# K and V made by the last pair of each gate phase, their memory lent to folds, kept parts and loads; T2 and B21 of the head k tile by k tile

## The chip, the cores and the metric

The kernel runs on one core of one Trainium2 chip. The metric is the device time of one execution in microseconds; it is given as a median of several runs. The core has five engines that run side by side and wait for each other by semaphores: PE (TensorE, matrix products, which write to the PSUM banks), DVE (VectorE), ACT (ScalarE), POOL (GpSimd), and SP (SyncE, which here only issues DMAs). Each engine works through its own queue in order, so an instruction that waits holds up what is queued behind it on its engine.

## The reference

One layer of a decoder trunk over 2048 rows of width 1024:

```python
mod = jax.nn.silu(c) @ w_ada[l] + b_ada[l]
shift, scale, gate = jnp.split(mod, 3, axis=-1)
u = x * (1.0 + scale[:, None, :]) + shift[:, None, :]
h = u @ w_in[l]
q, k, v, a_gate, p_in, p_gate, m_a, m_p = jnp.split(h, offsets, axis=-1)
a = sliding_window_sink_attention(q, k, v, sinks[l], bias, mask) * jax.nn.silu(a_gate)
a = a @ w_attn_proj[l]
p = jnp.einsum('bsgc,gcd->bsgd', multiscale_causal_pool(p_in), w_pool_mix[l]).reshape(B, S, POOL_WIDTH)
p = (p * pool_scale[l]) * jax.nn.silu(p_gate)
p = p @ w_pool_proj[l]
y = jax.nn.sigmoid(m_a) * a + jax.nn.sigmoid(m_p) * p
y = (y @ w_out[l]) * (1.0 + gate[:, None, :])
x = layer_norm(DEEPNORM_ALPHA * x + y, ln_gain[l], ln_bias[l])
```

Attention has 16 query heads, 2 key and value heads of width 64 (so K and V are 128 columns each of `h`), and a causal window of 128 rows. All arrays are float32.

## The kernel before

**Precision and products.** A float32 operand is split into a high part (rounded, type fp32r, made by an ACT copy) and a low part (the rest, made by a DVE subtraction, the helper `low`, line 131). A product is three matmuls: high by high, high by low, low by high (`mm3`).

**Sets and quads.** The 2048 rows are worked in two halves of 1024 rows (s = 0, 1), and each half as two column chunks of 512. Large products go by seven block products in place of eight (a Strassen-Winograd scheme). The moving side is kept as seven *sets* of four k tiles, each k tile split: B11, B21, B22 (blocks of u), and the sums T1, T2, T3, T4. The stationary side is a *quad* (class `Quad`): two column blocks of weights, 2 x 1024 wide, loaded into a buffer W (three thirds; two buffers) and a buffer A22 (two buffers in a common pool, and two of the phase's own that every other group uses). POOL makes the sums of weights (`sum1` line 283, `mid` lines 287 to 289, `late` line 293). A quad is worked in two steps. `front` splits the first pair of weights and does B11 and T1. `back` splits the second pair and does T2 and B21, splits the third pair and does T3 and B22, and last T4. `pair_split` (line 315 is its ACT copy, line 131 its DVE subtraction) writes to two of the four `w_set` slots, a ring; a slot comes free when the matmuls that read it are done. Each of the four result blocks goes to the quad's `consume`.

**Gate phases.** The gate phase of a half makes K, V and the gates: 17 quads, worked in groups of two (`gate_quads`); one late group has a single quad. `ring` runs the groups: `back` of a group, then `front` of the next. After each product it calls `tick`, and hooks given for a group and a position (`steps`, `at`) emit other work there: a full group has 14 ticks, ten in `back` and four in `front`. In the first phase the hooks are: the fold of the pool weights (`fold_parts`, for four groups: fetch, split, products, keep: `w_pool_mix` is folded into the pool columns of `w_in`, and stored), the sets of the second half (`sums_to`: x is loaded into two `spare` tiles, modulated, summed on POOL, split part by part into `k_hi` and `k_lo`, and stored), the last part of the modulation (`gate_modulation`) and the spreading of the bias. The fold's split also takes two `w_set` slots per half. `spare` is a ring of two tiles; `k_hi`, `k_lo`, gates and other pieces share the ring `c` of five.

**K and V.** The quad of K and V is the first of each phase. K is copied and split into the tile `kk` by `take_k` (line 651 its ACT copies, 64 partitions each), with four copies and four subtractions per chunk. V is kept as `vt`, and turned by PE into the tile `vv` in `turn_v`, emitted as `turn(0)` and `turn(1)` at hooks of group 0. The last piece of a phase, `first_q`, makes the first block of q for both chunks; then attention for that half begins, and it reads `kk` and `vv`. Attention also works on the first pair of the next phase at its end (`fill_one`).

**The head.** `head` runs before the first phase. For each of eight k tiles k it loads the modulation weights and x, makes shift (small PE products) and scale (a DVE reduction) in `opening(k)`, modulates x (`modulate_x`), writes the parts of B11 or B21 (`middle(k)`), and of T1 or T2 (`closing(k)`). B11 and T1 of the first two quads are done k tile by k tile as the parts come (`products`); T2 and B21 of these quads come later, in `back` of group 0. `rest_sums` makes the raw sums for T3 and T4; their parts and those of B22 are split in three hooks (`rest`) at group 0, positions 0, 1 and 3. The memory of `kk` and `vv` (18 KB and 9 KB per partition) holds weights and x of the head at first (`head_kk`, `head_vv`).

**What sets the order.** Operations on `pe`, `act`, `dve`, `pool` and `sp` keep the order of the program among themselves; those on `nc.scalar`, `nc.vector` and the like are placed by the planner of the framework by its own estimate of what is ready. The planner also puts in the waits. Memory that a pool gives out under one name again is given when its last users are done.

## Time and profile before

| | us |
|---|---|
| median of 3 runs | 1823.36 (1822.94 to 1827.17) |
| the profiled execution | 1824.69 |
| its span | 1822.9 |
| PE busy in the span | 1722.4 |
| DVE busy | 1315.4 |
| ACT busy | 933.8 |
| POOL busy | 929.5 |

The head lasts until about 73 us, the first gate phase until 439, the first attention until 706, the second gate phase from there to about 1040, the second attention to about 1322, and the projections and the output product take the rest. A line of the timeline gives start, duration (both in us), engine, line of the kernel, operation, output and inputs, shape, how many instructions are taken together, and in brackets the idle time ahead of it with what ended it. L55 is the line of the wrapper through which all operations on `pe`, `act`, `dve`, `pool` and `sp` go. A line of the waits gives the total in us, the number of waits, and the longest. The names `set_B` and `set_T` stand for all sets of that letter.

### The profile page before, as it was taken

The numbers are of one execution on the slowest core, as the hardware profiler recorded it, in microseconds if no ns is written. First come the engines' busy times: TensorE is split into PE (matmuls) and PEld (weight loads), VectorE is DVE, ScalarE is ACT, GpSimd is POOL, SyncE is SP. The second block draws the span as 40 slices with busy tenths as digits, with TensorE's granted clock in tenths as the row PEclk, the third lists the DMA queues.
The fourth block names the chain that finished last, engine by engine and source line by source line (L and its number), as shares of the span: only waits on it lengthen the run. The fifth ranks groups of instructions, "written<-read, shape, count | busy, mean of one in ns | idle before, by whom it ended". The sixth has DMA issues, their size and how long they took to land. (4 is left out here: it accounts for less than half of the span.)

```text
span 1822.9 us, 25301 instructions
## 1 busy us (share of the span) xinstructions
PE 1722.4 (94%) x8248; PEld 1432.9 (79%) x8248; DVE 1315.4 (72%) x2290; ACT 933.8 (51%) x1965; POOL 929.5 (51%) x758
## 2 busy tenths in 40 slices
PE   6789899999999999999999999999989999999996
PEld 6678787878888887777777888888877778777775
DVE  6967676644777787787666467777848897877887
ACT  4644344445777776444444377777724343423451
POOL 2245454551356567635445125357744875576552
PEclk9899999999999999999999999999999999999998
DMA  9265667656344468676676724453876575688442
GB/s 358 94 213 184 224 218 236 241 208 168 122 162 145 165 223 299 234 262 242 243 262 236 254 80 148 156 172 129 300 271 220 196 254 184 211 312 349 150 156 87
DMA packets 164003, 381.32 MB, mean 209 GB/s; under 512 B 19728, under 2 KB 23840, under 8 KB 163872
## 3 DMA queue, kind: packets, MB, share of 16 engines
q1 hardware_dynamic: 150528, 342.17, 53.7%
q0 software_dynamic: 10112, 33.06, 5.2%
q10 hardware_dynamic: 3232, 4.49, 0.9%
q8 instruction: 65, 1.06, 0.2%
q14 instruction: 66, 0.54, 0.1%
HBM read 244.35 MB, written 138.44 MB: 210 GB/s over the span
## 5 line engine op out<-in xcount | busy, mean ns | idle before, releaser
L55 PE MATMUL mm<-set_B,w_set 128*128 128x512 f32 x3240 | 802.1, 396 | 22.2 <-DVE w_set L131 22.0
L55 PEld LDWEIGHTS mm<-set_B,w_set 128*128 128x128 f32 x3240 | 602.9, 189 | 154.0 <-DVE w_set L131 30.3
L55 PE MATMUL lg<-set_T,w_set 128*128 128x512 f32 x2088 | 521.9, 400 | 44.3 <-DVE w_set L131 16.7
L55 PEld LDWEIGHTS lg<-set_T,w_set 128*128 128x128 f32 x2088 | 396.0, 192 | 146.2 <-DVE w_set L131 27.0
L131 DVE TENSOR_TENSOR w_set<-W,w_set 128x1024 fp32r<-128x1024 f32 x162 | 241.9, 1493 | 130.3 <-ACT w_set L315 125.6
L315 ACT CAST w_set<-W 128x1024 fp32r<-128x1024 f32 x162 | 169.2, 1049 | 242.5 <-PE mm L55 134.1
L55 PE MATMUL mm<-set_T,w_set 128*128 128x512 f32 x1080 | 266.4, 395 | 0.0
L55 PEld LDWEIGHTS mm<-set_T,w_set 128*128 128x128 f32 x1080 | 201.3, 189 | 41.6
L293 POOL TENSOR_TENSOR W<-W 128x512 f32<-128x512 f32 x56 | 80.0, 1429 | 151.0 <-DVE w_set L131 142.3
L287 POOL TENSOR_TENSOR W<-W 128x512 f32<-128x512 f32 x56 | 87.2, 1556 | 125.2 <-DVE w_set L131 99.9
L366 POOL TENSOR_TENSOR p<-p,u 128x512 f32<-128x512 f32 x58 | 100.6, 1736 | 87.3 <-DVE u L365 79.4
L55 DVE TENSOR_TENSOR o<-pv,o 64x128 f32<-64x128 f32 x256 | 72.4, 283 | 93.2 <-ACT o L55 90.5
L55 ACT ACTIVATE L<-L,nm 128x257 f32<-128x257 f32 (+1 forms) x256 | 127.1, 498 | 8.4 <-DVE nm L55 3.3
L283 POOL TENSOR_TENSOR W<-W,A 128x512 f32<-128x512 f32 x56 | 82.7, 1476 | 86.9 <-DMA W<-in_win_dram 20.2
L55 DVE TENSOR_TENSOR k_lo<-spare,k_hi 128x512 fp32r<-128x512 f32 x88 | 92.4, 1058 | 47.8 <-ACT k_hi L55 24.0
L55 DVE CUSTOM_DVE_ANT_0 L<-lg,bt,nsink 128x256 f32<-128x256 f32 (+1 forms) x256 | 111.6, 473 | 5.3 <-PE lg L55 1.3
L288 POOL TENSOR_TENSOR W<-W 128x512 f32<-128x512 f32 x56 | 90.4, 1614 | 15.1 <-DMA W<-in_win_dram 12.3
L55 POOL TENSOR_TENSOR w_set<-W,w_set 128x1024 fp32r<-128x1024 f32 x14 | 33.7, 2405 | 122.8 <-ACT w_set L55 89.7
L55 POOL TENSOR_TENSOR p<-nxt,pg 128x512 f32<-128x512 f32 x32 | 41.3, 1291 | 104.6 <-DVE sm L55 104.6
L55 ACT COPY o<-pv 64x256 f32<-64x256 f32 x128 | 47.3, 370 | 82.3 <-PE pv L55 80.2
L55 DVE TENSOR_TENSOR ptl<-pt,pth 128x512 fp32r<-128x512 f32 (+1 forms) x128 | 85.7, 669 | 1.7 <-ACT pth L55 1.6
L55 ACT CAST k_hi<-spare 128x512 fp32r<-128x512 f32 x88 | 53.4, 615 | 60.4 <-POOL spare L55 32.3
(207 smaller groups left out, 2507.2 us busy)
## 6 DMA issues: line engine op xcount, KB each, us to landing
W<-in_win_dram SPq DMA_DIRECT2D x68, 256.0 KB, 4.1
w_set<-wmix_d SPq DMA_DIRECT2D x32, 512.0 KB, 5.4
A<-in_win_dram SPq DMA_DIRECT2D x34, 256.0 KB, 5.1
W<-in_win_dram POOLq DMA_DIRECT2D x34, 256.0 KB, 3.6
ag_d<-sig SPq DMA_DIRECT2D x32, 256.0 KB, 3.5
pg_d<-sig SPq DMA_DIRECT2D x32, 256.0 KB, 3.6
ma_d<-sig SPq DMA_DIRECT2D x32, 256.0 KB, 4.1
mp_d<-sig SPq DMA_DIRECT2D x32, 256.0 KB, 3.7
```

The source lines that it names most:

```text
L55: return lambda *args, **kw: self.tc.keep_in_program_order(op(*args, **kw))
L131: engine.tensor_tensor(dst, src, as32(hi), ALU.subtract)
L283: e.tensor_tensor(self.w[:, 1, :], self.w[:, 2, :], self.a22, ALU.add)
L287: e.tensor_tensor(x[:, 1, :], x[:, 1, :], x[:, 0, :], ALU.subtract)
L288: e.tensor_tensor(x[:, 2, :], x[:, 0, :], x[:, 2, :], ALU.subtract)
L293: e.tensor_tensor(x[:, 0, :], x[:, 0, :], x[:, 1, :], ALU.subtract)
L315: a.copy(by_two(hi), raw)
L366: nc.gpsimd.tensor_tensor(p5, p5, u2, ALU.add)
```

## The change

The quad of K and V goes from the first place of a gate phase to the last group, beside the last gate quad. Group 0 is then two quads of the attention gate. `turn(0)` is emitted at position 7 of the last group, `turn(1)` inside `first_q`, between its two products. In the first phase the memory of `kk` and `vv` is a set of rooms until then: the fold's splits of the weights are written there and no more to `w_set`; two of three kept parts (`k_hi`, `k_lo`) go there and no more to the ring `c`; and two more `spare` tiles are taken there, in turn with the two of the ring. `place_kv` ends that when the first block of K is consumed. The fold of a group has its products two ticks behind its splits. The ticks of folds, of the first sums and of the gate modulation are shifted.

In the head, the second pairs are split earlier, and T2 and B21 of both quads are done as their k tiles come. The copies of two results (`u2`, `p5`) are made there too. The parts of T3 are split in the head, those of B22 and T4 at positions 4 and 6 of group 0, and the `late` sum of the second quad at position 4.

```diff
         def split():
-            t.extend(ph.c(n, F32R) for n in ("k_hi", "k_lo"))
+            at = ph.turn_of("parts")
+            if at:
+                t.extend(cols(rooms["k"], n + 2) for n in at)
+            else:
+                t.extend(ph.c(n, F32R) for n in ("k_hi", "k_lo"))
...
-        for q, (a, b, c, w) in zip(grp, opened):
-            u2, p5 = ph.p("u2"), ph.p("p5")
-            nc.scalar.copy(u2, a)
-            nc.scalar.copy(p5, b)
+        for q, (a, b, c, w, *copies) in zip(grp, opened):
+            if copies:
+                u2, p5 = copies
+            else:
+                u2, p5 = ph.p("u2"), ph.p("p5")
+                nc.scalar.copy(u2, a)
+                nc.scalar.copy(p5, b)
...
-            product(a, w[0], "B21")
+            if not copies:
+                product(a, w[0], "B21")
...
             if mi == 0:
+                if s == 0 and t == 0:
+                    place_kv(ph)
                 take_k(s, t, src)
...
             part((hi, lo), 0, KT)
+            if not accs:
+                turn(1)
...
-            w[:] = ph.split(), ph.split()
+            w[:] = (cols2(rooms["k"], n) for n in range(2))
...
-            (3, lambda: fold(0)),
-            (4, lambda: (keep(), split(1))),
-            (5, lambda: fold(1)),
-            (6, keep),
+            (4, lambda: fold(0)),
+            (5, lambda: (keep(), split(1))),
+            (7, lambda: fold(1)),
+            (8, keep),
...
-        quads = [kv]
+        quads = []
...
-        groups = [quads[i : i + 2] for i in range(0, 14, 2)] + [quads[14:15], quads[15:17]]
+        groups = [quads[i : i + 2] for i in range(0, 14, 2)] + [quads[14:15], [kv, quads[15]]]
...
+        def second_pair(x):
+
+            o, u2 = opened[x], ph.p("u2")
+            o[2:] = bank("lg"), pair_split(ph, grp[x].second(), act, dve), u2
+            act.copy(u2, o[0])
+
+        def more(x, name, i0, i1):
+            a, b, c, w, _ = opened[x]
+            if name == "T2":
+                product(c, w[1], name, True, i0, i1)
+            else:
+                product(a, w[0], name, False, i0, i1)
+
         for k in range(2, KT):
             opening(k)
+            if k == 7:
+                second_pair(0)
             closing(k - 2)
...
+        more(0, "T2", 0, 2)
+        more(0, "B21", 0, 3)
         closing(6)
+        second_pair(1)
+        more(1, "T2", 0, 2)
+        more(1, "B21", 0, 3)
         middle(7)
-        opened[0][3] = pair_split(ph, grp[0].second(), act, dve)
         closing(7)
-        opened[1][3] = pair_split(ph, grp[1].second(), act, dve)
-        for i in (3, 2):
+        for x in range(2):
+            more(x, "T2", 2, 4)
+            more(x, "B21", 3, 4)
+        for i in (2, 3):
             rest_sums(i)
-        for q in grp:
-            q.late(dve)
-        dve.tensor_scalar(nsink, nsink, -1.0, None, ALU.mult)
+        for o in opened:
+            o.append(ph.p("p5"))
+            act.copy(o[5], o[1])
         late_sets(cp, "B22")
         late_sets(ph.t, "T3", "T4")
-        parts("T4", 1, xs[5][0])
+        for i in range(4):
+            parts("T3", i, xs[i][0])
+        grp[0].late(dve)
+        dve.tensor_scalar(nsink, nsink, -1.0, None, ALU.mult)
...
-            steps(hooks, groups, (13, 41, 69, 92)[g], fold_parts(ph, g))
-        for i in range(2):
-            at(0, (7, 10)[i], lambda i=i: turn(i))
+            steps(hooks, groups, (11, 39, 67, 91)[g], fold_parts(ph, g))
+        at(-1, 7, lambda: turn(0))
...
-            steps(hooks, groups, (1, 29, 57, 80)[i], todo)
+            steps(hooks, groups, (4, 29, 57, 80)[i], todo)
...
-            steps(hooks, groups, 28 * (i // 2) + 20 + i % 2, gate_modulation(ph, 2 * KT + i, cb))
-        for n, f in zip((0, 1, 3), rest):
+            steps(hooks, groups, (21, 49, 77, 99)[i // 2] + i % 2, gate_modulation(ph, 2 * KT + i, cb))
+        at(0, 4, lambda: groups[0][1].late(dve))
+        for n, f in zip((4, 6), rest):
             at(0, n, f)
...
-        hooks = {(0, (8, 10)[i]): [lambda i=i: turn(i)] for i in range(2)}
+        hooks = {(-1, 7): [lambda: turn(0)]}
...
+    def place_kv(ph):
+
+        nonlocal kk, vv
+        ph.turns.clear()
+        kk = kvp.tile([P, 2, 2, P + 2 * CH], F32R, tag="kk", name="kk")
+        vv = kvp.tile([P, 2 * NB + 1, 2, P], F32R, tag="vv", name="vv")
...
-        kk = kvp.tile([P, 2, 2, P + 2 * CH], F32R, tag="kk", name="kk")
-        vv = kvp.tile([P, 2 * NB + 1, 2, P], F32R, tag="vv", name="vv")
+        rooms["k"] = kvp.tile([P, 4 * (P + 2 * CH)], F32R, tag="kk", name="room_k")
+        rooms["v"] = kvp.tile([P, 2 * (2 * NB + 1) * P], F32, tag="vv", name="room_v")
+        ph.turns["spare"] = cycle([None, None] + [cols2(rooms["v"], n) for n in range(2)])
+        ph.turns["parts"] = cycle([(2, 3), (4, 5), None])
```

More of the change, by code (lines that the diff above doesn't have):

```diff
@@ L2 @@
 from contextlib import ExitStack
+from itertools import cycle
 import numpy as np
@@ L147, in __init__ @@
         def __init__(self, name, **bufs):
-            self.name, self.bufs = name, bufs
+            self.name, self.bufs, self.turns = name, bufs, {}
         def __enter__(self):
@@ L166, in split, with turn_of @@
             return wp.tile([P, D], F32R, tag="wset", bufs=4, name="w_set")
+        def turn_of(self, ring):
+            return next(self.turns[ring]) if ring in self.turns else None
         def spare(self, dt=F32):
+            room = self.turn_of("spare")
+            if room is not None:
+                return room
             return self.t.tile([P, D], dt, tag="spare", bufs=self.bufs["spare"], name="spare")
@@ L688, in moving_u, with first_q @@
         return (sets["B11"], sets["B21"]), (sets["T2"], sets["B22"])
-    def first_q(ph, tick):
+    def first_q(ph, turn):
         raw, hi, lo = ph.spare(), ph.split(), ph.split()
@@ L1259, in first_phase @@
             at(-1, 3 + half, lambda half=half: build(ph, "T2", half, b12_d))
-        return ring(ph, groups, opened, hooks, [], lambda tick: first_q(ph, tick))
+        return ring(ph, groups, opened, hooks, [], lambda tick: first_q(ph, turn))
     def second_phase(ph, opened, groups, turn):
-        hooks = {(0, (8, 10)[i]): [lambda i=i: turn(i)] for i in range(2)}
+        hooks = {(-1, 7): [lambda: turn(0)]}
         for p, name, half in ((0, "T3", 0), (1, "T3", 1), (3, "T4", 0), (5, "T4", 1)):
@@ L1294, in second_phase, with cols2 @@
             hooks.setdefault((-1, 3 + half), []).append(lambda half=half: fill_set("T2", half, u1_d["B12"]))
-        return ring(ph, groups, opened, hooks, [], lambda tick: first_q(ph, tick), True)
+        return ring(ph, groups, opened, hooks, [], lambda tick: first_q(ph, turn), True)
     def pairs(make):
         return [[make(m), make(m + 2)] for m in (0, 4)]
+    rooms = {}
+    kk = vv = None
+    def place_kv(ph):
[3 more added lines that the diff above has]
+        vv = kvp.tile([P, 2 * NB + 1, 2, P], F32R, tag="vv", name="vv")
+    def cols2(t, n):
+        return t[:, n * D : (n + 1) * D]
     kv_stack = ExitStack()
```

8 lines of the change are left out of this document (2 added, 6 removed).

## The prediction

> **What bounds the kernel now.** The page comes first, for the busiest engine; then stretches of the span, to see where that engine is not busy; then the waits of that engine; then the timeline around them.
>
> ```profile
> span 1822.9 us, 25301 instructions
> PE 1722.4 (94%) x8248; PEld 1432.9 (79%) x8248; DVE 1315.4 (72%) x2290; ACT 933.8 (51%) x1965; POOL 929.5 (51%) x758
> ```
>
> PE (TensorE) is busy 94% of the span; the change adds and removes no product, so only PE's 100 us of idle time, and matmuls at a lowered clock, can be won. They are not spread evenly:
>
> ```profile
> 0.00:60.00 60.00, 40.39 (x194) 35.91 (x195) 41.99 (x105) 32.11 (x50) 13.17 (x46) 0.91 0.72 272
> 60.00:90.00 30.00, 24.55 (x98) 19.66 (x97) 26.44 (x35) 14.90 (x25) 12.68 (x7) 0.89 0.37 132
> ```
>
> After the time of a stretch stand the busy us of PE, PEld, DVE, ACT and POOL, then the granted clock. From 60 to 90 us PE lacks 5.5 us while DVE is busy for 26.4 of 30, and the clock is 0.89: there DVE is the bound. For the gate phase behind it, the waits of PE from 92 to 440 us (total us, times, longest):
>
> ```profile
> PE lg L55 <- ACT w_set L315: 7.7, 6, 2.3
> PE lg L55 <- DVE w_set L131: 3.7, 8, 0.5
> PE mm L55 <- DVE w_set L131: 2.4, 2, 1.2
> PE pv L55 <- DVE w_set L55: 0.8, 1, 0.8
> PE pv L55 <- ACT w_set L55: 0.4, 1, 0.4
> ```
>
> PE waits for weight splits (w_set) only. Most of these waits, all but those of the third row, lie beside the folds of the pool weights. A usual split and one beside a fold:
>
> ```profile
> 406.05 1.05 ACT L315 CAST w_set<-W 128x1024 fp32r<-128x1024 f32 x1 [4.08 <-PE mm L55]
> 411.47 2.93 PE L55 MATMUL lg<-set_T,w_set 128*128 128x512 f32 x12
> ...
> 110.40 1.04 ACT L55 CAST w_set<-spare 128x1024 fp32r<-128x1024 f32 x1 [2.04 <-PE mm L55]
> 111.83 1.05 ACT L315 CAST w_set<-W 128x1024 fp32r<-128x1024 f32 x1
> ...
> 112.93 1.09 PE L55 MATMUL lg<-set_T,w_set 128*128 128x512 f32 x2 [2.33 <-ACT w_set L315]
> 114.19 3.63 PE L55 MATMUL lg<-set_T,w_set 128*128 128x512 f32 x10 [0.17 <-DVE w_set L131]
> 125.65 2.57 PE L55 MATMUL lg<-set_T,w_set 128*128 128x512 f32 x10 [0.52 <-DVE w_set L131]
> ...
> 204.34 3.88 PE L55 MATMUL lg<-set_T,w_set 128*128 128x512 f32 x10 [0.53 <-DVE w_set L131]
> ```
>
> Usually ACT begins a pair's third split when PE lets go of the slots of the first quad's second split (406.05), 5.4 us before PE needs it (411.47). Beside a fold, the fold's split (110.40, from `spare`) has taken those two of the four w_set slots; the third split (111.83) comes behind it, on slots that PE frees only as it gets to the point where it needs the result. So PE stands for one ACT copy and part of one DVE subtraction. The head, on PE and then on DVE:
>
> ```profile
> 46.08 1.84 PE L55 MATMUL lg<-ct,head_kk 128*128 128x1 f32 x16
> 52.15 1.22 PE L55 MATMUL lg<-set_T,w_set 128*128 128x512 f32 x2 [4.22 <-ACT w_set L55]
> 54.57 4.38 PE L55 MATMUL lg<-set_T,w_set 128*128 128x512 f32 x10 [1.20 <-DVE w_set L55]
> 73.05 4.63 PE L55 MATMUL lg<-set_T,w_set 128*128 128x512 f32 x10 [5.45 <-DVE w_set L131]
> 77.48 3.59 PE L55 MATMUL mm<-set_B,w_set 128*128 128x512 f32 x12
> ...
> 92.39 2.93 PE L55 MATMUL mm<-set_B,w_set 128*128 128x512 f32 x12
> ```
>
> ```profile
> 47.20 1.28 DVE L55 CUSTOM_DVE_ANT_0 head_kk<-head_kk,cb,mod 128x1024 f32<-128x1024 f32 x1
> 60.46 1.29 DVE L55 TENSOR_TENSOR set_T<-spare,set_T 128x512 fp32r<-128x512 f32 x2
> 71.78 1.22 DVE L131 TENSOR_TENSOR w_set<-W,w_set 128x1024 fp32r<-128x1024 f32 x1
> ```
>
> The wait that ends last in the head is that for the third split of the first quad, a DVE subtraction at 71.78; what lies ahead of it in DVE's queue sets the time.
>
> **The change part by part.**
>
> *Head, T2 and B21 k tile by k tile; K and V gone from the first pair.* Up to DVE's 47.20 nothing changes. Then DVE has, ahead of that third split: two second splits (1.22 less the 0.08 by which neighbours overlap, 1.14 each), 22 subtractions or adds of 512 columns (two take 1.29 where one takes 0.69, so 0.60 each: three T2 lows, two differences, two B21 lows, six rest sums, four T3 lows, one late sum, two u2, two gate products), and the split itself at 1.14. From 48.5 that is 2.3 + 13.2 + 1.1 = 16.6, so T3 of the first quad can begin at 65.2. This holds if the four B22 lows, the four T4 lows and the second late sum (nine, 5.4 us), which the code now puts behind it, really come behind; if they come first, it is 70.6. The order is the planner's and the trace can't show it; I take the middle, 68.0, for before it let B22 and T4 lows and K's four lows come first. Against 73.05 this is **5.0 us less** (2.4 to 7.9). The earlier T2 and B21 don't count besides: PE gets to the same wait sooner and stands longer. What is late next is again this wait. Everything up to the front of the next pair (92.39) moves with it; V's transposes go from here to the end of the phase, at the same cost.
>
> *Folds in their own rooms.* The fold's split leaves the w_set ring, and the fold comes two ticks behind its split. The first, second, fourth and fifth rows of the waits go: **12.6 us less**. The cover is the 5.4 us that ACT and DVE then have for a split of 1.05 + 1.2; where fold work of more than 3 us gets between, the wait is back. Half of it, 6.3, is the lower end, and all of it gone the upper; I take all, since the four folds show the same order of slots. With the waits go slowed matmuls: ten at 114.19 took 3.63 and at 204.34 3.88, where 125.65 has 2.57; that is 1.06 + 1.31, **2.4 us less**. The Trainium skill, "TensorE: Matmul & The Clock Gate", section "What's actually happening", lets the clock fall only after an idle window of about 3.4 us; the 4.63 us for ten after 5.45 us of waiting agrees, the two rows after waits of 2.33 and less don't. By the page this term would be nothing and the time 1812; I go by the rows.
>
> *Kept parts in rooms, spare ring of four.* Fewer waits for stores:
>
> ```profile
> 105.95 0.62 ACT L55 CAST k_hi<-spare 128x512 fp32r<-128x512 f32 x1 [3.74 <-DMA u_T_split<-k_hi]
> 190.72 2.56 PE L55 MATMUL mm<-set_B,w_set 128*128 128x512 f32 x10 [1.19 <-DVE w_set L131]
> ```
>
> ACT waits there for its own store, PE mostly doesn't notice. The 2.4 us of the third row of waits (190.72 is one of the two) come while kept parts are made; they may go (2.4 less) or stay. But the first fold now stands on the same ticks as the first kept parts (4 to 18 against 11 to 19; before, 1 to 15 and 13 to 19). I take one more such wait and none less: **1.2 us more** (from 2.4 less to 2.4 more).
>
> *The last fold.* It starts at tick 91, not 92, but is a tick longer where it matters: its second half ran in the single-quad group ahead of T3, now behind it. It holds both A22 buffers which the next pair, K and V, is loaded into.
>
> ```profile
> 380.41 0.81 SPq L277 DMA_DIRECT2D A<-in_win_dram  x2
> ...
> 384.46 1.28 POOL L283 TENSOR_TENSOR W<-W,A 128x512 f32<-128x512 f32 x1 [1.07 <-DMA A<-in_win_dram]
> ...
> 385.77 1.05 ACT L315 CAST w_set<-W 128x1024 fp32r<-128x1024 f32 x1 [4.24 <-POOL W L283]
> ...
> 386.85 1.35 DVE L131 TENSOR_TENSOR w_set<-W,w_set 128x1024 fp32r<-128x1024 f32 x1 [2.74 <-ACT w_set L315]
> ...
> 388.66 2.93 PE L55 MATMUL mm<-set_B,w_set 128*128 128x512 f32 x12
> ```
>
> From the load (on SP's queue, whose later issues wait with it) to the end of the split is 7.8 us, and it ended 0.5 before PE took it. One product later (2.75), less the 1.1 that PE waited at this fold, the load goes at 382.1 and the split ends at 389.9; PE is due at 388.66 - 1.1 = 387.6. **2.0 us more** (0 to 2.3, as two of twelve matmuls need only the copy).
>
> *K and V in the last pair, both phases.* The work is the same, moved:
>
> ```profile
> L651 ACT CAST kk<-mm x8: 575/581/585, 61.7 to 722.8; 64x512 fp32r<-64x512 f32 x8
> L131 DVE TENSOR_TENSOR kk<-mm,kk x8: 672/689/695, 65.9 to 723.4; 64x512 fp32r<-64x512 f32 x8
> ```
>
> The four copies and four subtractions of one K half alternate on one PSUM bank: 4 x (0.58 + 0.69) = 5.1 us, in which the third split has to find its place on ACT and DVE, in a stretch where it has 3 us to spare. If the planner puts it between them nothing is lost; if it comes last PE waits 5.1 + 1.05 + 1.2 - 5.4 = 2.0. I take **1.0 more in each phase**. V's second transposes stand between the two q products of 5.4 us each, and the first scores need K alone; that cover holds.
>
> The sum: -5.0 - 12.6 - 2.4 + 1.2 + 2.0 + 1.0 + 1.0 = -14.8. The profiled execution took 1824.69 (span 1822.9), 1.3 over the median; 1824.7 - 14.8 = **1810**.
>
> **The rivals.** *The gains are eaten* (half the fold waits stay because ACT and DVE are late anyway, the head's order comes out at 70.6): -2.4 - 6.3 - 1.2, and the new waits at their upper ends, 2.3 + 2.0 + 2.0 + 2.4, make -1.2, so 1823.5. For it speaks that DVE has 26.4 of 30 us in the head; against it that each fold wait begins when PE frees a slot and not when ACT gets free.
>
> *K's chain costs at the end what it cost at the start*: in the old first group the wait was 5.45, and the slow clock added 2.1 (4.63 against 2.57) and 0.7 (3.59 against 2.93); twice 8.2 in place of twice 1.0 gives 1824, no change. Against it, the same chain in the second phase's first group:
>
> ```profile
> 711.19 11.07 PE L55 MATMUL mm<-set_B,w_set 128*128 128x512 f32 x48
> ...
> 717.76 0.58 ACT L651 CAST kk<-mm 64x512 fp32r<-64x512 f32 x1
> 717.77 1.23 DVE L131 TENSOR_TENSOR w_set<-W,w_set 128x1024 fp32r<-128x1024 f32 x1 [0.87 <-ACT w_set L315]
> ```
>
> The third split stands between two kk copies there, and PE runs 48 matmuls without a wait.
>
> *The rooms are followed as one tile*, so that each write into a room waits for the last store out of it: slower. 21 kept pairs and 8 fold splits, each with ACT standing up to 3.74 us; if each of the 29 passes 1.0 us of it on to PE, the time is 1810 + 29 = 1839; it decides from 0.65 us on, where 1829 is reached, 0.3% above the median. Against it, parts of one head tile are read and written together:
>
> ```profile
> 41.52 1.84 PE L55 MATMUL lg<-ct,head_kk 128*128 128x1 f32 x16
> 42.92 1.28 DVE L55 CUSTOM_DVE_ANT_0 head_kk<-head_kk,cb,mod 128x1024 f32<-128x1024 f32 x1
> ```
>
> DVE writes one part of `head_kk` while PE reads another, without a wait.
>
> **How the numbers follow.** 0.3% (5.5 us) is about what a measurement of this kernel can tell from no change. The forecast has 0.72, eaten gains 0.10, K's chain 0.07, the rooms 0.11. The forecast's own range is 1800 (head -7.9, third row gone, no new waits) to 1818; to leave out no more than 2 in 10 the range goes on to 1825, over the first two rivals. Faster 0.74 (0.02 of the eaten gains still pass the bound), same 0.15, slower 0.11.
>
> **What the changed profile would show.** T3 of the first quad begins at 65 to 71; no fold split writes w_set, and PE's waits from the head's end to the first attention are under 6 us in place of 15; a wait of about 2 us at the front of the last pair; kk written near 400 and near 1000, with at most 2 us of PE waits beside each. Wrong it would be through ACT waits on stores in the rooms, or through new waits for `w_set` behind the kk copies.

## The result, and the profile after

The changed kernel takes 1824.87 us (median), the kernel before, beside it on the same chips, 1825.73. The ratio of the two, over all executions (not the quotient of the medians), is 1.0002 with a 95% interval of 0.999 to 1.0015: no difference. Forecast were 1810 us and a range from 1800 to 1825; the gain of 15 us did not come.

The profiled execution of the changed kernel took 1827.73 us, 2.9 above its median; that of before, 1824.69, was 1.0 below the median of the runs beside. So the choice of the two executions alone puts 3.9 us between them; the spans are 3.0 apart. The page of after, its first lines; PE is as busy as before:

```profile
span 1825.9 us, 25285 instructions
PE 1722.9 (94%) x8248; PEld 1431.7 (78%) x8248; DVE 1328.6 (73%) x2290; ACT 932.7 (51%) x1965; POOL 938.6 (51%) x758
```

PE does the same 8248 matmuls in nearly the same order; 6408 of them have 512 columns. The n-th of these, counted from 0 and called product n from here on (one matmul, not the three of `mm3`), can be set beside the n-th of the other trace. The table shows how much earlier (minus) or later the changed kernel starts it, in us, and what each stretch of the span added:

| up to product (its start before) | stretch | after stands at | added here | forecast |
|---|---|---|---|---|
| 200 (100.7) | head | -2.3 | -2.3 | -5.0 |
| 1176 (362.0) | three folds, kept parts | -12.4 | -10.1 | -12.7 |
| 1272 (391.4) | last fold, front of the last pair | -8.2 | +4.2 | +0.9 |
| 1344 (408.7) | last pair, gate row stored | -4.4 | +3.8 | 0 |
| 1464 (436.3) | K's copies, to the end of the phase | -3.5 | +0.9 | +1.0 |
| 2184 (679.3) | first attention | -2.8 | +0.7 | 0 |
| 3696 (1058.0) | second gate phase | +5.9 | +8.7 | +1.0 |
| end of span | the rest | +3.0 | -2.9 | 0 |

The last row is code that the change doesn't touch. (The forecast's -12.6, -2.4 and +1.2 are split here: -1.1 of the first belongs to the last fold.) By 362 us the change had won 12.4 us. It lost 8.0 in the next 47 us, and the rest in the second gate phase.

The stretch between products 200 and 1176, as windows of before (first fence) and after, and behind it the stretches that follow in after; columns as in the prediction:

```profile
100.50:362.00 261.50, 248.31 (x1123) 201.39 (x1121) 173.60 (x191) 108.11 (x162) 127.95 (x106) 0.99 0.64 219
```

```profile
98.40:349.60 251.20, 242.92 (x1122) 199.73 (x1121) 179.21 (x182) 108.08 (x162) 134.50 (x108) 1.00 0.67 234
...
376.00:384.00 8.00, 5.55 (x17) 4.10 (x17) 6.16 (x6) 3.84 (x5) 7.84 (x5) 0.79 0.19 74
384.00:398.00 14.00, 12.97 (x58) 10.40 (x56) 3.07 (x3) 2.02 (x3) 4.52 (x5) 1.00 0.25 44
398.00:406.00 8.00, 6.25 (x20) 4.74 (x21) 6.29 (x6) 5.45 (x7) 3.67 (x3) 0.79 0.17 66
```

In the three folds PE idles 8.3 us in place of 13.2, and the same products keep it busy for 5.4 us less: half of what was won is clock (0.99 to 1.00). Then come two holes, at 376 to 384 and 398 to 406, each with the clock at 0.79. The timeline of after at the first hole, the last fold and the front of the last pair behind it:

```profile
370.43 0.82 SPq L288 DMA_DIRECT2D A<-in_win_dram  x2
375.47 1.26 POOL L294 TENSOR_TENSOR W<-W,A 128x512 f32<-128x512 f32 x1 [2.58 <-DMA A<-in_win_dram]
376.76 1.04 ACT L326 CAST w_set<-W 128x1024 fp32r<-128x1024 f32 x1 [5.62 <-POOL W L294]
377.86 0.73 PE L56 MATMUL mm<-set_B,w_set 128*128 128x512 f32 x2 [1.83 <-ACT w_set L326]
379.21 4.15 PE L56 MATMUL mm<-set_B,w_set 128*128 128x512 f32 x10 [0.62 <-DVE w_set L132]
```

And at the second, the store of the gate row (an `nc.scalar` DMA, in single elements of 4 bytes; the code emits it in `gate_rows`, a hook of group 0 of the second phase, and the planner issues it here) and the load of the last pair behind it:

```profile
385.88 0.40 ACTq L1308 DMA_DIRECT2D gate_d<-mod  x1
387.28 0.57 POOL L300 DMA_DIRECT2D W<-in_win_dram  x1 [0.30 <-POOL W L298]
398.13 1.04 ACT L326 CAST w_set<-W 128x1024 fp32r<-128x1024 f32 x1 [8.01 <-DMA W<-in_win_dram]
399.22 0.73 PE L56 MATMUL lg<-set_T,w_set 128*128 128x512 f32 x2 [2.25 <-ACT w_set L326]
400.48 4.00 PE L56 MATMUL lg<-set_T,w_set 128*128 128x512 f32 x10 [0.52 <-DVE w_set L132]
406.93 0.58 ACT L668 CAST kk<-mm 64x512 fp32r<-64x512 f32 x1 [0.75 <-DVE kk L132]
407.04 2.93 PE L56 MATMUL lg<-set_T,w_set 128*128 128x512 f32 x12
408.03 1.04 ACT L326 CAST w_set<-W 128x1024 fp32r<-128x1024 f32 x1
```

The load issued at 387.28 lets ACT go at 398.13, 10.8 us later. Behind it K's copies stand with a third split between them (408.03), and PE runs on.

Two traces of one kernel differ too. A second profile of before (`b1_before_again`, below) runs 2.3 to 4.5 us later than the first between products 200 and 2350, and the second gate phase adds another 2.5. The two profiles of `m1` (below) differ by 5.8 us between products 200 and 1176. So a difference of this size in one pair of traces shows nothing by itself; where an effect is that small, the text below goes by the medians or by several traces.

### The profile page after: what moved, and what is told of

The parts are those of the page before. It is cut to its first block, busy times and chain, and to the rows that moved or that the text cites. A ratio compares the mean times of both kernels' runs of the same rounds, so it can differ in the third digit from the quotient of the medians.

```text
span 1825.9 us, 25285 instructions
## 1 busy us (share of the span) xinstructions
PE 1722.9 (94%) x8248; PEld 1431.7 (78%) x8248; DVE 1328.6 (73%) x2290; ACT 932.7 (51%) x1965; POOL 938.6 (51%) x758
## 5 line engine op out<-in xcount | busy, mean ns | idle before, releaser
L56 PE MATMUL lg<-set_T,w_set 128*128 128x512 f32 x2088 | 518.8, 398 | 39.8 <-DVE w_set L132 12.7
L298 POOL TENSOR_TENSOR W<-W 128x512 f32<-128x512 f32 x56 | 89.5, 1599 | 142.1 <-DVE w_set L132 110.9
L304 POOL TENSOR_TENSOR W<-W 128x512 f32<-128x512 f32 x56 | 82.8, 1480 | 152.0 <-DVE w_set L132 144.4
L380 POOL TENSOR_TENSOR p<-p,u 128x512 f32<-128x512 f32 x58 | 96.4, 1663 | 68.5 <-DVE u L379 64.0
L294 POOL TENSOR_TENSOR W<-W,A 128x512 f32<-128x512 f32 x56 | 86.2, 1539 | 85.6 <-DMA A<-in_win_dram 15.3
L299 POOL TENSOR_TENSOR W<-W 128x512 f32<-128x512 f32 x56 | 92.9, 1659 | 16.3 <-DMA W<-in_win_dram 13.3
L56 DVE TENSOR_TENSOR k_lo<-spare,k_hi 128x512 fp32r<-128x512 f32 x61 | 68.1, 1120 | 39.8 <-ACT k_hi L56 23.2
L56 PE MATMUL lg<-kk,qs 128*128 128x256 f32 (+1 forms) x512 | 80.5, 279 | 0.0
```

Of the source, the lines that this page charges most:

```text
L56: return lambda *args, **kw: self.tc.keep_in_program_order(op(*args, **kw))
L294: e.tensor_tensor(self.w[:, 1, :], self.w[:, 2, :], self.a22, ALU.add)
L298: e.tensor_tensor(x[:, 1, :], x[:, 1, :], x[:, 0, :], ALU.subtract)
L299: e.tensor_tensor(x[:, 2, :], x[:, 0, :], x[:, 2, :], ALU.subtract)
L304: e.tensor_tensor(x[:, 0, :], x[:, 0, :], x[:, 1, :], ALU.subtract)
L380: nc.gpsimd.tensor_tensor(p5, p5, u2, ALU.add)
```

## The experiments

The theories after the first comparison: *the store of the gate row* makes the last load late (for it, 387.28 to 398.13); *the last fold* holds the A22 buffers too long; *K and V at the end* cost in the second phase what K's chain cost at the start; *the new head* is worth nothing. The rival to all of them was that the middle of the phase is crowded, so that any wait removed comes back elsewhere.

**The store of the gate row.** `e1_gate_store_late`: the store is issued by ACT in the last group.

```diff
-            nc.scalar.dma_start(gate_d.rearrange("k p -> p k"), mod[:, 16:24], ...)
...
+        at(-1, 6, lambda: act.dma_start(
+            gate_d.rearrange("k p -> p k"), mod[:, 16:24], ...))
```

> The changed kernel, with one edit: the store of the gate row (1024 elements of 4 bytes, issued on ACT's queue at 385.9 us in the changed kernel, right ahead of the load of the last pair's second weights) is tied to position 6 of the last group, about where it ran in the kernel before (411.8). Theory A (this store holds up other DMAs for some 9 us, and in the changed kernel that hits the load issued at 387.3, which landed at 398.0): the 2.25 + 0.52 us wait of PE near 399 and the slow matmuls behind it go, the first score of attention comes 4 to 5 us earlier (431 in place of 435.5), and the whole is up to 5 us faster than the changed kernel if nothing later takes it back. Rival B (the load is late for its own reasons: its issue behind POOL's sums, or DMA traffic): the load still needs about 10 us, and the first score stays near 435.

1822.44 us, ratio to before 0.9984 (0.9971 to 0.9996). From product 1272 to 1344 this kernel goes from -8.3 to -9.3 where after went from -8.2 to -4.4: 4.8 us in the trace, 2.4 between the medians, whose intervals just overlap. (`e3_both` and `e2_last_fold_earlier` below also differ by this edit alone: 1822.63 and 1831.56, with intervals apart.) The view of transfers in the stretch 384 to 400 us, after and then this kernel (name, size, median us from issue to landing):

```profile
DMA packets 1255, 0.62 MB, mean 39 GB/s; under 512 B 1088, under 2 KB 1088, under 8 KB 1254
...
q10 hardware_dynamic: 1040, 0.00, 3.5%
...
W<-in_win_dram POOLq DMA_DIRECT2D x2, 256.0 KB, 6.8
gate_d<-mod ACTq DMA_DIRECT2D x1, 4.0 KB, 8.7
```

```profile
W<-in_win_dram POOLq DMA_DIRECT2D x2, 256.0 KB, 2.8
W<-in_win_dram SPq DMA_DIRECT2D x1, 512.0 KB, 3.3
```

With the store away, the pair's two loads land in 2.8 us in place of 6.8 (the mean of an early one and the late one). The store itself goes later, and there it is as slow and its neighbours as late, but PE waits for none of them. The transfers of this kernel from 404 to 417 us:

```profile
A<-in_win_dram SPq DMA_DIRECT2D x2, 256.0 KB, 9.9
gate_d<-mod ACTq DMA_DIRECT2D x1, 4.0 KB, 11.7
```

`g1_gate_row_turned`: the row is turned by PE and stored as eight rows.

```diff
+            pe.transpose(turned, mod[:, 16:24], ident)
+            row = ph.t.tile([KT, P], F32, tag="grow", bufs=1, name="grow")
+            act.copy(row, turned)
+            act.dma_start(gate_d, row)
...
+        at(-1, 5, gate_row)
```

> The changed kernel; the gate row is turned by PE at position 5 of the last group (128 x 8 to 8 x 128) and stored in 8 rows of 512 bytes in place of 1024 elements of 4 bytes. The work added is one PE transpose, one ACT copy, one DMA. Theory A (the small elements hold the DMA queues for 9 to 12 us): the store lands within 3 us, loads issued around it land in 3 to 5 us, the wait near 399 goes, the first score is near 430.5 as with the late store, and the time is 1822 or a little under, as loads near 410 no longer wait either. Rival B (any store at that place does it): as with the late store or no better than the changed kernel.

1821.79 us, 0.998 (0.9963 to 0.9996), as with the late store. The transfers from 409 to 424 us: 16 packets in place of 1040, and the loads of A beside them land in 2.8 us, other loads of the stretch in 3.8 to 5.7.

```profile
q10 hardware_dynamic: 16, 0.00, 0.1%
...
A<-in_win_dram SPq DMA_DIRECT2D x2, 256.0 KB, 2.8
```

So it is the form of the store that makes its neighbours late, and its place that lets PE feel it. Both kernels have the last fold as after has it.

**The last fold.** `e2_last_fold_earlier` starts it a tick earlier, `e3_both` does that beside `e1`'s edit.

```diff
-            steps(hooks, groups, (11, 39, 67, 91)[g], fold_parts(ph, g))
+            steps(hooks, groups, (11, 39, 67, 90)[g], fold_parts(ph, g))
```

> The changed kernel, with the fourth fold started one tick earlier (90 in place of 91), so that its second half runs ahead of T3 in the single-quad group, as in the kernel before. Theory A (both A22 buffers come free a product too late for the load of the last pair): the wait of 1.83 + 0.62 us of PE at the front of the last pair, and the slow matmuls behind it, go; 2 to 4.5 us earlier there. Rival B (front late for POOL's sum or DVE's order): the wait stays. In either case the wait near 399 may stay, since the gate row's store is not moved.

> Both edits, the late store of the gate row and the earlier fourth fold. If both causes hold, the first gate phase gives 12 us (first score near 427 to 428 against 439.0 before). Theory A on the rest: the second gate phase's first group is held by the loads of T3 and T4 whenever it starts early, so at most 2 to 4 of these 12 us are seen in the time: 1821 to 1824. Rival B: the gain passes through and the time is 12 us under before, 1813.

1831.56 us, 1.0027 (1.0007 to 1.0048), and 1822.63, 0.9985 (0.9974 to 0.9996). The wait at the front of the last pair fell only from 1.83 + 0.62 us to 0.67 + 0.62 in `e2` and stood at 1.18 + 0.63 in `e3`; in `e2` waits of 1.02, 0.40 and 0.52 us came up beside the fold, and the last load, again late beside the gate row's store, made PE wait for 3.95. A tick earlier moves the wait, and doesn't remove it. That `e2` is 7 us slower than after is not accounted for in full by these waits.

`m1_fold_mix_in_room` removes the need: `e1`, and the fold's mixing matrix goes from the two A22 buffers to the room of `kk`, which one of the two kept parts there gives up.

```diff
-                for n in ("mhi", "mlo"):
-                    m.append(wp.tile([P, CH], F32R, tag="A22", bufs=2, name=n))
+                m.extend(cols(rooms["k"], n) for n in (6, 8))
...
-        ph.turns["parts"] = cycle([(2, 3), (4, 5), None])
+        ph.turns["parts"] = cycle([(2, 3), None])
```

> The late store of the gate row, and the fold's own split weights (mhi, mlo) in the room of kk in place of the two common A22 buffers; one of the two rooms of kept parts is given up for it. Theory A (the last pair's A22 load waits for the fold to let go of A22): the load is issued some 10 us earlier, the wait of 1.9 us at the front of the last pair and the slow matmuls behind it go, and the first score comes 3 to 4.5 us earlier than with the late store alone (430.6), near 427; time 1818 to 1820. Rival B (the front waits for POOL's sum or for DVE): it stays near 430.

1816.57 us, 0.9943 (0.9924 to 0.9961); beside later kernels (`m1_again`) 1815.88, 0.995 (0.9931 to 0.9969).

> The kernel with the late gate store and the fold's mix weights in the room of kk, again, beside the next one on the same chip: 1816 to 1819, ratio to before 0.994 to 0.997.

In the timeline of `m1_again` the load goes out at 356.12 us, where after has 370.43, and in its windows PE is busy without a break:

```profile
356.12 0.43 SPq L288 DMA_DIRECT2D A<-in_win_dram  x1
```

```profile
376.00:384.00 8.00, 8.00 (x37) 6.63 (x36) 2.65 (x4) 2.71 (x4) 4.11 (x3) 1.00 0.23 83
384.00:394.00 10.00, 10.00 (x45) 8.27 (x45) 4.87 (x6) 5.23 (x7) 2.57 (x2) 1.00 0.07 20
```

From product 1176 to 1272 it adds nothing (-15.0 to -15.1), in the first profile of `m1` 0.9. In `e1`, where the mix still stands in the A22 buffers, the same stretch adds 3.2 (-11.5 to -8.3), in after 4.2. Between the medians of this kernel and `e1` (1822.44) lie 6 us. What the edit gives besides lies ahead of product 1176: from product 200 to there the seven traces with the mix in the room win 8.3 to 16.1 us (mean 12.9), the seven with the changed first phase and the mix in the A22 buffers 7.2 to 10.6 (mean 8.6). The cause of this part isn't settled.

**Is the middle of the phase crowded?** `c1_first_fold_later` is `m1` with the first fold moved away from the first kept parts.

```diff
-            steps(hooks, groups, (11, 39, 67, 91)[g], fold_parts(ph, g))
+            steps(hooks, groups, (15, 39, 67, 91)[g], fold_parts(ph, g))
```

> The same kernel (late gate store, mix weights in the room), with the first fold four ticks later (15 in place of 11), so that it shares fewer ticks with the first kept parts (8 to 18). Theory A (the waits of some 4 us between 130 and 150 us, at the third split and front of the second group, are crowding by the fold on top of kept parts): they fall to 1 us or less, and the phase ends 2 to 3 us earlier. Rival B (they come from the kept parts, modulation and DVE alone): they stay within 1 us in sum.

1816.22 us, 0.9944 (0.9928 to 0.9961), the time of `m1`. PE's waits from 92 to 340 us are 5.1 us, against 8.7 in the first profile of `m1` and 4.6 in the second: chance. Nothing speaks for the theory here: fewer ticks shared by the first fold and the first kept parts gained nothing.

**K and V at the end of the second phase.** `e5_second_kv_first` is after with K and V at the front of the second phase, as before the change; `p1_second_kv_first` does it to `m1`.

```diff
-        quads = []
+        quads = [kv] if s else []
...
-        hooks = {(-1, 7): [lambda: turn(0)]}
+        hooks = {(0, (8, 10)[i]): [lambda i=i: turn(i)] for i in range(2)}
```

> The changed kernel, but in the second gate phase K and V stand first again and are turned in group 0, as before the change; the first phase and the head are those of the changed kernel. Theory A (moving K and V in the second phase costs 5 to 9 us between 700 and 1060): the time is 5 us or more under the changed kernel, near 1819. Rival B (the second phase loses its lead at the loads of T3 and T4 in group 0 in any order, and what differs behind it is chance): within 2 us of the changed kernel, and the second attention starts with the same lead or lag as there.

> The same kernel with K and V first again in the second gate phase. Theory A (K and V last in the second phase costs 4 to 8 us): 1811 to 1814, 4 us or more under the same kernel with K and V last. Rival B (what the second phase lost is chance and the loads at its start): within 2 us of it.

1823.63 us, 0.9987 (0.9976 to 0.9998), and 1811.38, 0.9916 (0.9894 to 0.9937), 4.5 to 5.2 us less than `m1`. The 1.2 us between `e5` and after are not told apart by their intervals, and those of `p1` and `m1` overlap a little; that two more kernels built on `p1` (below) take 1812.06 and 1810.11 stands beside it. From product 2184 to 3696 nine traces with K and V last take 3.5 to 8.7 us longer than the first trace of before (mean 6.0), and the seven with K and V first, that trace itself among them, -0.8 to 5.6 (mean 1.6). So K and V last go with some 4 us, and the 8.7 of after's trace are partly chance. PE's waits in this phase, total, times and longest, `m1_again` and then `p1`:

```profile
PE lg L56 <- DVE w_set L132: 5.5, 8, 1.5
PE mm L56 <- DVE w_set L132: 5.0, 4, 1.5
PE lg L56 <- ACT w_set L326: 3.2, 3, 2.3
```

```profile
PE lg L56 <- DVE w_set L132: 4.1, 7, 1.2
PE mm L56 <- DVE w_set L132: 3.7, 3, 1.4
PE lg L56 <- ACT w_set L326: 2.2, 3, 1.6
```

The difference, 3.7 us in these rows, lies in waits for splits over the whole phase; no wait stands at K's copies. In group 0, from which K and V are gone, one wait tells the two orders apart: at products 2340 and 2342 PE waits for a split in all nine traces with K and V last, for 0.9 to 1.5 us and 0.5 more, and in none with K and V first. In `m1_again`:

```profile
716.07 0.70 PE L56 MATMUL lg<-set_T,w_set 128*128 128x512 f32 x2 [0.92 <-ACT w_set L333]
717.23 1.20 PE L56 MATMUL lg<-set_T,w_set 128*128 128x512 f32 x4 [0.46 <-DVE w_set L132]
```

One cause would be that group 0 now stores four gate blocks more. `x1_second_fewer_stores` is `m1` without the stores of one quad of the second phase; the first phase stores that quad's blocks twice in their place:

```diff
-            defer(2, lambda: sp.dma_start(gates_d[name][s, m + mi, t], g))
+            to = (0, 1) if (s, name, m) == (0, "ag", 2) else (s,)
+            if (s, name, m) == (1, "ag", 2):
+                return
+            for z in to:
+                defer(2, lambda z=z: sp.dma_start(gates_d[name][z, m + mi, t], g))
```

> The kernel with the late gate store and the mix weights in the room (K and V last in both phases). Left out: in the second half the second quad of the attention gate is not stored; its place is filled from the first half (stored twice in the first phase), so the second half's result uses wrong gates for those columns. So the first group of the second phase has four stores of 256 KB in place of eight, as many as with K and V first. Theory A (the four more stores among the loads of T3 and T4 cost the 3 us): the stretch from the second products of that group to its end is 2 to 4 us shorter than in m1_again, near that of p1. Rival B (order of DVE and ACT work there): less than 1 us shorter.

1812.76 us, 0.9919 (0.9898 to 0.994): 3 to 4 us under `m1`, with intervals that overlap, and near `p1`, though K and V stay last. From product 2184 to 3696 it adds 2.1 us, as the kernels with K and V first do. In its trace the wait at product 2340 is gone; behind it, at product 2346, PE waits longer for a load:

```profile
719.45 2.81 PE L56 MATMUL lg<-set_T,w_set 128*128 128x512 f32 x11 [2.26 <-DMA set_T<-u_T_split]
```

So from product 2310 to 2350 `x1` still loses 3.5 us. That net loss doesn't tell the orders apart: it is 3.0 in `m1_again` and 4.7 in after, but also 2.5, 2.8 and 3.5 in `e5`, `x3` and `x2` with K and V first, where PE waits for loads of parts of sets; the 0.9 of `p1` is an exception. So the stores bear on the price of K and V last, one wait of 1.4 to 2.0 us in group 0 among it. How much of the 4 us is theirs isn't shown: `x1` has four stores fewer in the whole second phase, which no kernel with K and V first has, and was run four times.

**The head.** `h1_head_alone` is the kernel before with the new head alone (the rows are from the hunk of `head`, the rest as in the change); `r1_rooms_old_head` is after with the old head, and `x3_best_old_head` is `p1` with the old head.

```diff
+            if k == 7:
+                second_pair(0)
...
+        more(0, "T2", 0, 2)
+        more(0, "B21", 0, 3)
...
-        for i in (3, 2):
+        for i in (2, 3):
```

> The kernel before with the new head alone: T2 and B21 k tile by k tile, the copies u2 and p5 and the T3 parts in the head, B22 and T4 parts at positions 4 and 6. K and V stay first, folds stay in the w_set ring, all other ticks are as before. Theory A (the head's gain of 4.7 us at the front of the second group is the head's own, and is kept by the phase): the second attention phase and the end come 3 to 5 us earlier, the time is 1821 to 1822. Rival B (DVE is the bound up to 100 us, so the head alone only moves the wait, and K's four copies in group 0 take it back): less than 2 us, near 1825.

> The changed kernel with the old head: K and V last in both phases, rooms for folds, kept parts and loads; T2 and B21 in group 0 as before, the second pairs split after the last k tile. Theory A (folds gain 8 us, the last pair and the single-quad group give 9 back, the second phase loses some 3 more): the time is 1827 to 1830, slower than before and 4 us slower than the changed kernel. Rival B (head and rooms overlap, the same DVE time is saved twice): as the changed kernel, near 1825.

> The kernel p1 (late gate store, mix weights in the room, K and V first in the second phase) with the old head. Theory A (the new head is worth its 4.7 us at the front of the second group, to the end): 1815 to 1816. Rival B (DVE is the bound to 100 us and the lead is gone by the second group): within 1.5 us of p1.

`h1` takes 1831.55 us, 1.0028 (1.001 to 1.0046): slower. `r1` takes 1827.91, 1.0004 (0.9983 to 1.0024), not told apart from after. `x3` takes 1810.11, 0.991 (0.9892 to 0.9928), and `p1` with the new head 1811.38. At product 168, the front of the second group (92.4 before), the traces stand: after -4.7, `p1` -4.5, `x3` -4.6 with the old head, `r1` -1.2, and `h1` +8.4 (in an execution 7 us above its median). In `h1` K's quad is still in group 0, and PE waits for parts of sets at 88 and 93 us:

```profile
88.42 0.80 PE L55 MATMUL lg<-set_T,w_set 128*128 128x512 f32 x1 [4.87 <-ACT set_T L55]
92.60 8.35 PE L55 MATMUL lg<-set_T,w_set 128*128 128x512 f32 x23 [3.38 <-DVE set_T L55]
```

`h1` carries the whole new head, with the parts of T4 split at position 6 and no more at 3; which part of it loses beside K isn't separated. Where K and V leave group 0, the lead that is left at product 200 is there with the old head too: 5.0 in `x3` and 2.2 in `r1`, and 0 to 3.4 in the twelve traces with the new head. T2 and B21 k tile by k tile add nothing that these runs can tell.

`x3` and `r1`, whose heads are the same code, stand 3.4 us apart at product 168; 2.9 of these are a matter of the clock. Behind a wait of 2.81 us the next ten and twelve matmuls of `r1` take 4.63 and 3.74 us, and behind one of 3.13 those of `x3` take 2.57 and 2.89.

**What was left over.** `x2_best_gate_row_turned` is `p1` with `g1`'s turned row, and `b1_before_again` is the kernel before, unchanged, with a second profile.

> The changed kernel with the mix weights in the room, K and V first in the second phase, and the gate row turned by PE and stored in 8 rows. Theory A (the small elements hold the queues near 410 too, and loads of the first attention wait there): 1 to 3 us under p1, 1808 to 1810. Rival B (nothing on PE's path waits for a DMA there): as p1, 1811.

> The kernel before, unchanged, for a second profile of it. Between the last products of the first attention and the start of the second, the changed kernel's profile lost 8.7 us against the first profile of before. Theory A (this is the cost of K and V in the last pair of the second phase): the second profile of before takes that stretch in the same time as the first, within 1 us. Rival B (the stretch varies from execution to execution by several us): it is 2 to 5 us longer than in the first.

1812.06 us, 0.9921 (0.99, 0.9943), the time of `p1`: once it is issued late, the store in single elements costs nothing more that the medians show. Before again: 1826.14, 0.9998 (0.9982 to 1.0014). Its trace gave the size of chance used above. The best kernels, `p1` and `x3`, are 0.8 to 0.9% faster than before and than after. The trace of `p1` that the text uses is of an execution of 1803.32 us, 8 below its median, so its leads (-16.9 at product 1176) are likely upper ends.

## Why the prediction was wrong

In short: the gate row's store had no term (+3.8), the last fold's term left out the clock and a new wait ahead of it (3.3 over the forecast), K and V in the second phase cost some 4 us in place of 1.0, the head's lead was not kept (2.7 short), and the fold stretch came 2.6 short. Of the signs of being wrong that the prediction names only one ACT wait of 0.8 us came: it failed at other places. (In its sum for the head, 48.5 and 16.6 make 65.1 and not 65.2, and the upper end of 1818 stands there without its sum; nothing below hangs on either.)

**The head, -5.0: it came where it was worked out, and was not kept.** T3 of the first quad begins at 65.54 us with two matmuls, and its other ten at 68.25, within the 65 to 71 forecast. The lead at these ten is 4.8 us, with the old head and K and V gone 0.8 (`r1`) and 1.5 (`x3`), so the new head moves this wait as forecast; at the front of the next pair it is 4.7. But the rows behind it, of after's timeline and then of its windows, show what "everything up to the front of the next pair moves with it" left out:

```profile
90.37 2.58 PE L56 MATMUL mm<-set_B,w_set 128*128 128x512 f32 x10 [2.10 <-DVE w_set L132]
96.91 2.58 PE L56 MATMUL mm<-set_B,w_set 128*128 128x512 f32 x10 [0.78 <-DVE w_set L132]
```

```profile
60.00:90.00 30.00, 22.19 (x83) 16.55 (x81) 28.10 (x37) 16.46 (x28) 8.44 (x6) 0.89 0.47 163
90.00:110.00 20.00, 18.85 (x91) 15.68 (x92) 18.59 (x16) 11.12 (x17) 12.21 (x10) 1.00 0.72 256
```

DVE is busy for 28.1 of 30 us and then 18.6 of 20, and PE waits for it: it stays the bound for 20 us longer than the step assumed, and by product 200 the lead is 2.3, no more than without the new head. The step that failed is that a lead at the front of the next pair lasts. By the code the nine operations moved behind T3 are still DVE's to do in group 0.

**The folds, -12.6 - 2.4 + 1.2: right in the mechanism, 2.6 short (by the seven traces above, 4).** No fold split writes `w_set`, and of the four rows of waits one wait of 1.8 us is left. The step failed in the term for new waits, +1.2. PE's waits of after in the stretch 98 to 350:

```profile
PE mm L56 <- DVE w_set L132: 5.0, 5, 1.3
PE lg L56 <- DVE w_set L132: 1.8, 1, 1.8
PE lg L56 <- DVE p L402: 1.5, 1, 1.5
```

8.3 us are left, where 13.3 - 11.5 + 1.2 = 3.0 were forecast: waits for DVE's share of a split, and one for a block of output. The step put such waits down to the first fold on the same ticks as the first kept parts; `c1`, which moves it away from them, gained nothing, so what makes DVE late there stays open. The clock gave 3.0 more than the 2.4 of the step (5.4). That term was put down from two rows alone. From 92 to 440 us PE's waits come to 15.3 us in both kernels, and "under 6" was forecast.

**The last fold, +2.0 less the 1.1 of its old wait: came as 3.2 to 4.2.** Place and mechanism were right, and the 1.83 + 0.62 us of waiting are near the 2.0 forecast. The step left out the clock, though a term for it stood two paragraphs above: the ten matmuls at 379.21 took 4.15 us in place of 2.57. And the 1.1 saved at the fold were taken back by a wait of 1.09 us for a block of output, at 364.64. The windows of after show where the clock fell:

```profile
376.30:379.70 3.40, 1.22 (x4) 0.74 (x5) 1.86 (x2) 1.58 (x2) 3.32 (x3) 1.00 0.21 81
379.70:383.10 3.40, 3.40 (x10) 2.63 (x9) 3.40 (x4) 1.68 (x2) 3.32 (x3) 0.50 0.06 22
```

By the Trainium skill, "TensorE: Matmul & The Clock Gate", section "What's actually happening", the clock falls after an idle window of about 3.4 us. The length agrees with the 3.4 us at 0.50. Read as a window that is idle throughout it doesn't agree, for PE was busy for 1.22 us of the one ahead.

**The store of the gate row: no term for it, +3.8.** By `e1` the store costs 4.8 us in the trace, and 1.0 was won beside it. The change moved the ticks of `gate_modulation`, the last of them to an earlier place; the text ahead of the prediction names this, and the sum gives it no price. The store behind it is on `nc.scalar`, so by the code the planner can issue it once the modulation is ready: it goes at 385.88 where it stood at 411.82. No run moves these ticks back alone. Before, it held up a load as well, which PE didn't need. The transfers of before from 412 to 424 us:

```profile
spare<-in_win_dram SPq DMA_DIRECT2D x1, 512.0 KB, 11.0
gate_d<-mod ACTq DMA_DIRECT2D x1, 4.0 KB, 12.1
```

So the row that would have priced it stood in the trace of before. A forecast has to follow each moved step to its DMA, its queue and what shares the transfer engines with it then.

**K's chain, +1.0 in each phase.** In the first phase the chain cost nothing: there is no wait at the copies, by the mechanism forecast. That the stretch adds 0.9 us, near the 1.0 forecast, is luck: it stands in all fourteen traces with K and V last there, and is V's eight transposes (0.11 us each), which the forecast moved at no cost. In the second phase K and V last cost some 4 us, in waits for splits and not at the chain. The reasoning looked only at the place to which K and V go. It gave no price to what comes forward in their place, the gate quad's stores above all, with which one wait in group 0 comes and goes; the rest of the 4 us stays open.

**The rivals.** The rooms followed as one tile would have made 29 ACT waits; one of 0.8 us stands in the trace, at 88 us, and the phase gained. K's chain costing 8.2 is refuted in the first phase. Eaten gains, 1823.5, comes nearest the time, but by other mechanisms than it named: 12.4 us were won, and then lost at two places, where the clock added 1.6 and 1.4 us to waits of 2.45 and 2.77, and in the second phase.

The sum by what was measured: -2.3 - 10.1 + 4.2 + 3.8 + 0.9 + 4 (second phase, by several traces) = +0.5, no change, as the medians say. It mixes one pair of traces with a mean of several, so the closeness is in part chance.

## What to carry to other kernels

Before a step is moved, follow every instruction in it that the framework may place by itself, small stores above all, to the transfers that it will then stand beside. Memory lent to one user is lent by the next one too: ask when its first load behind the loan has to go out. And a wait of PE of 2 to 3 us can cost some 1.5 us more by the clock behind it; two such places ate 8 of 12 us here. Compare several traces before a stretch is given a cause: the loss of group 0 looked like the price of K and V last until the kernels with K and V first showed it too.

## What the runs showed of the hardware

A store of 4 KB in 1024 single elements takes 8.7, 11.7 and 12.1 us to land in three kernels and moves its 1040 packets on a queue that is busy for 3.5 to 4.9% of those stretches. Loads of 256 and 512 KB issued on other queues beside it land 7.1 to 12.6 us after their issue, where loads in the stretches without it (384 to 400 us of before, of `e1` and of `g1`) land in 2.8 to 4.4. As eight rows it is 16 packets, and loads beside it land in 2.8 to 5.7 us. The Trainium skill, "DMA: Bandwidth & Descriptors", section "Rules for kernel authors", says that a strided last dimension lowers to one descriptor per element, and in "Issuing engines are not separate DMA queues" that transfers of all issuing engines interleave on the same engines. The 1040 packets agree with the first, and the late loads on other queues with the second.

The clock of after stands at 0.50 from 379.7 to 383.1 and from 400.2 to 403.6, 3.4 us each, and at 1.00 around them. In the 3.4 us ahead of each, PE was busy for 1.22 and 0.91 us, and the waits there come to 2.45 and 2.77. A longer wait need not do it: behind the 3.13 us of `x3` (68.4 to 71.6) the clock stays at 1.00, and this wait lies across two such stretches:

```profile
66.80:70.20 3.40, 1.64 (x8) 1.02 (x6) 3.40 (x7) 1.53 (x2) 3.21 (x2) 1.00 0.86 284
70.20:73.60 3.40, 2.02 (x9) 1.69 (x10) 2.46 (x2) 0.00 (x0) 0.24 (x1) 1.00 0.64 228
73.60:77.00 3.40, 3.40 (x17) 2.79 (x16) 1.99 (x3) 0.89 (x2) 1.77 (x2) 1.00 0.91 304
```

So in these traces the idle share of a single stretch of 3.4 us goes with the fall, and where a wait falls among the stretches is in part chance.
